# The last norm of a two-layer encoder: its sums, weights and stores taken apart

## The chip, the cores and the metric

The kernel runs on one core of one Trainium2 chip. The metric is the device time of one execution in microseconds (us). The kernel before takes 1240.49 us (median of 3 runs, 1240.41 to 1240.75).

## The reference

The input is x, 256 tokens of 2048 features. Layer 0 is a pre-norm layer with differential attention and a spatial gating branch, layer 1 a pre-norm recurrent layer; both add a residual. The change touches only what follows the last product:

```
y = (h * silu(z_c)) @ c_w_out          # 256 x 2688 times 2688 x 2048
x = x + y
return x * rsqrt(mean(x * x, axis=-1) + 1e-6) * final_norm
```

So each token needs the sum of the squares of all its 2048 features before any of its output can be scaled.

## The kernel before, in words

All weights stream from memory in the order of use, as chunks that are cut into units of up to eight 128x128 tiles. A unit is loaded by the queue of SP (`load`, line 204, tile `raw`), split by ACT into a high part (`split_hi`, `hi`) and by DVE into a low part (`split_lo`, `lo`), and multiplied by PE as three products (lines 337 to 339). Loads run six units ahead of the splits, and the splits up to six units ahead of the products.

`run(emit)` writes the program of one chunk s. `at(s, fn, ph)` puts other work into a chunk's program: phases -1 to 0.5 around the splits, 1 and 1.5 behind them, 2 behind the products. Each engine executes its own instructions in the order in which they were written, so a helper's place in that order decides what it waits behind. A DMA that SP or ACT issues is an instruction of that engine's queue too.

The last product, `out_product("co", KC, x2_done)`, goes over four blocks of 512 features (cb 0 to 3), each block as two accumulators, one for each half of the tokens (t = 0 and 1, 128 tokens on the 128 partitions). In the last chunk the products of t = 0 come first and those of t = 1 after them. When a block is done, `res_add` (line 382, DVE) adds the residual into `res`, and `squares` (line 385, ACT) squares the 512 features and leaves their sum in one column of `ssq`. For the first three blocks this runs beside the products of the next block, and `gf_mult` (line 986, DVE) multiplies the finished features by final_norm there. The weights of that norm, `gf`, are eight tiles of 256 features, which ACT's queue loads at chunk s1 + 8 (line 978), s1 being the first chunk of the last product.

The last block has no product behind it. For each half of the tokens the program does, in this order: `res_add`, `squares`, then `finish(t)`: DVE sums the four columns of `ssq` (line 362) and turns them into mean plus eps (line 366), POOL takes the power -1/2 (line 367), and then ACT scales features 0 to 511 and 512 to 1023 (line 1006), and DVE scales 1024 to 1535 (line 1008) and scales and weights the last 512 in two pieces of 256 (line 1012). SP stores four pieces of 512 features for each half (line 1013), eight stores in all.

Of the kernel before, what the change touches and what calls it, by code (L numbers as in the profile page):

```python
# [12 lines left out]
ALU = mybir.AluOpType  # L13
AX = mybir.AxisListType

P = 128
S = 256
NT = S // P
DM = 2048
# [7 lines left out]
EPS = 1e-6  # L27
# [43 lines left out]
def plan():  # L71

    chunks = []
    add = lambda kind, **kw: chunks.append(dict(kind=kind, **kw))
    for cb in range(4):
        for kq in range(4):
            add("vb", cb=cb, kq=kq, n=16)
    for ct in range(KD):
        add("u", ct=ct, n=16)
        add("zb", ct=ct, n=16)  # L80

    def heads(p):
        for h in (2 * p, 2 * p + 1):
            for j in range(2):
                add("q", h=h, j=j, n=16)
            for j in range(2):
                add("k", h=h, j=j, n=16)
        for kq in range(4):
            add("v", p=p, kq=kq, n=16)

    def za(p):
        for kq in range(4):
            add("za", p=p, kq=kq, n=16)

    def out(kind, rows):

        for cb in range(4):
            for k in range(0, rows - 3, 4):
                nk = rows - k if rows - k < 8 else 4
                add(kind, cb=cb, k0=k, nk=nk, n=4 * nk)  # L100

    heads(0)
    out("ob", KD)
    za(0)
    for p in range(1, H // 2):
        heads(p)
        za(p)
    out("oa", KD)

    early = [(j, k) for j in range(2) for k in range(12)] + [(j, k) for j in range(2) for k in range(12, KD)]  # L110
    xb = lambda jk: add("xb", jk=jk, n=16)
    xb(early[:16])
    xb(early[16:])
    for j in range(2, LEAD):
        xb([(j, k) for k in range(KD)])
    for j in range(KC):
        if j + LEAD < KC:
            xb([(j + LEAD, k) for k in range(KD)])
        for z in z_rows(j):
            add("zc", j=z, n=16)  # L120
        add("gt", j=j, n=2 * len(gate_tiles(j)))
    add("zc", j=KC - 1, n=16)
    out("co", KC)
    off = 0
    for c in chunks:
        c["off"] = off
        off += c["n"] * P * P
    return chunks, off
# [3 lines left out]
def trunk(ctx, tc, xT, xt, prm, rep, wsp, wst, out):  # L132
    nc = tc.nc
    V, A, T, GP, SP = nc.vector, nc.scalar, nc.tensor, nc.gpsimd, nc.sync
# [20 lines left out]
    mhalf = cpool.tile([P, NT], F32, name="mhalf")  # L155
    GP.memset(mhalf, -0.5)
    small = lambda n, w: cpool.tile([P, w], F32, name=n)
    rt, rh, nlam = small("rt", NT), small("rh", NT), small("nlam", 1)
# [7 lines left out]
    res = room.rearrange("p (t d) -> p t d", t=NT)  # L166
    ssq = small("ssq", NT * 4).rearrange("p (t c) -> p t c", t=NT)
# [22 lines left out]
    chunks, _ = plan()  # L190
# [70 lines left out]
    def at(s, fn, ph=0):  # L261


        assert (s, ph) > passed[0], (s, ph)
        todo.setdefault((s, ph), []).append(fn)
# [94 lines left out]
    def q_sum(ts=slice(0, NT)):  # L360

        V.tensor_reduce(rt[:, ts], ssq[:, ts, :], axis=AX.X, op=ALU.add)
        return rt[:, ts]

    def r_pow(ps, ts=slice(0, NT)):
        V.tensor_scalar(rt[:, ts], ps, 1.0 / DM, EPS, op0=ALU.mult, op1=ALU.add)
        GP.tensor_tensor(rt[:, ts], rt[:, ts], mhalf[:, ts], op=ALU.pow)
# [12 lines left out]
    def res_add(cb, pss, t):  # L380
        f = slice(cb * 512, (cb + 1) * 512)
        V.tensor_tensor(res[:, t, f], res[:, t, f], pss[t], op=ALU.add)

    def squares(cb, t):
        A.activation(sqs, res[:, t, cb * 512:(cb + 1) * 512], AF.Square, accum_out=ssq[:, t, cb:cb + 1])
# [69 lines left out]
    with tc.tile_pool(name="pb", bufs=2) as pb:  # L455
# [112 lines left out]
        for ct in range(KD):  # L568
            u = None
# [224 lines left out]
    with tc.tile_pool(name="pc", bufs=2) as pc:  # L794
        y.add(pc, KC - KD, "y2")
        tl = lambda n, j, b, dt=F32: pc.tile([P, S], dt, tag=n, name=f"{n}{j}", bufs=b)
# [176 lines left out]
        gf, s1 = [], pos[0]  # L973

        def gf_load():
            for a in range(DM // S):
                gf.append(tl("th" if a < 4 else "q", f"gf{a}_", 4))
                A.dma_start(gf[a], rep[:, GF + a * S:GF + (a + 1) * S])

        at(s1 + 8, gf_load)  # L980

        def gf_mult(cb):
            for t in range(NT):
                for a in (2 * cb, 2 * cb + 1):
                    r = res[:, t, a * S:(a + 1) * S]
                    V.tensor_tensor(r, r, gf[a], op=ALU.mult)

        def x2_done(cb, pss, s):
            if s < len(chunks) - 1:
                at(s + 1, lambda: [res_add(cb, pss, t) for t in range(NT)])  # L990
                at(s + 1, lambda: [squares(cb, t) for t in range(NT)], 1)
                at(max(s + 2, s1 + 10), lambda: gf_mult(cb), 1)
                return
            for t in range(NT):
                at(s, lambda t=t: (res_add(cb, pss, t), squares(cb, t), finish(t)), 2)

        def finish(t):


            ts = slice(t, t + 1)  # L1000
            r_pow(q_sum(ts), ts)
            sc = rt[:, ts]
            for n, (a, b) in enumerate(((0, 512), (1024, 1536), (512, 1024), (1536, 2048))):
                r = res[:, t, a:b]
                if n % 2 == 0:
                    A.activation(r, r, AF.Copy, scale=sc)
                elif b < DM:
                    V.tensor_scalar_mul(r, r, sc)
                else:
                    for c in range(a, b, S):  # L1010
                        r = res[:, t, c:c + S]
                        V.scalar_tensor_tensor(r, r, sc, gf[c // S], op0=ALU.mult, op1=ALU.mult)
                SP.dma_start(out[:, t, a:b], res[:, t, a:b])

        out_product("co", KC, x2_done)


# [89 lines left out]
```

## Time and profile before

| what | us |
|---|---|
| median of 3 runs | 1240.49 |
| the profiled execution | 1240.98 |
| its span, first to last instruction | 1239.2 |
| PE busy | 1228.1 (99% of the span) |
| DVE busy | 844.1 |
| ACT busy | 673.6 |
| POOL busy | 34.9 |

The span is the time between the first and the last instruction that the profiler recorded; the 1.8 us between it and the execution's time lie around it. A time in a row is counted from the span's start. An engine's busy time is an average over the whole program: PE is busy for 99% of it, and yet the last stretch, in which PE has nothing left to do, is ruled by other engines.

### The profile page before, as it was taken

How to read it: one execution, taken by the hardware profiler on the slowest of the kernel's cores; microseconds unless marked ns; L12 is line 12 of the kernel's file. 1: busy time of each engine (PE TensorE's matmuls, PEld its weight loads, DVE VectorE, ACT ScalarE, POOL GpSimd, SP SyncE). 2: the span in 40 equal slices, each digit the busy share in tenths (PEclk: the TensorE clock that was granted, in tenths of full speed). 3: DMA queues.
4: the chain of work that ended last, by engine and by line, in shares of the span. 5: the costliest groups of instructions: out<-in, count | busy, mean ns of one | idle time of the engine just before them, and what ended most of it. 6: DMA issues, size and time to landing. Idle time of an engine off the chain costs nothing.

```text
span 1239.2 us, 17358 instructions
## 1 busy us (share of the span) xinstructions
PE 1228.1 (99%) x6458; PEld 1056.9 (85%) x6458; DVE 844.1 (68%) x1304; ACT 673.6 (54%) x1083; POOL 34.9 (3%) x66
## 2 busy tenths in 40 slices
PE   9999999999999999999999999999999999999997
PEld 7888888888888888888888888888989989898885
DVE  6847777777556656746646655557899999988553
ACT  7544444454444334444544544455788788877442
POOL 1100000000000000000000000000000000000000
PEclk9999999999999999999999999999999999999999
DMA  9855665555645565555555555455566666656651
GB/s 329 278 188 170 238 202 173 186 187 176 213 156 187 193 196 172 187 170 174 184 174 167 191 174 179 170 189 172 202 192 198 215 205 203 207 179 228 223 178 68
DMA packets 70981, 237.66 MB, mean 192 GB/s; under 512 B 8176, under 2 KB 9840, under 8 KB 70640
## 3 DMA queue, kind: packets, MB, share of 16 engines
q1 hardware_dynamic: 66960, 228.76, 55.4%
q10 hardware_dynamic: 2016, 4.64, 1.1%
q0 software_dynamic: 1920, 3.15, 1.0%
q8 instruction: 51, 0.84, 0.3%
q14 instruction: 34, 0.28, 0.1%
HBM read 231.27 MB, written 2.10 MB: 188 GB/s over the span
## 4 chain that ended last, share of the span: by engine, by line
PE 98%; DMA 1%; DVE 0%; SPq 0%; issue 0%; ACT 0%; ACTq 0%; POOLq 0%; POOL 0%; DVEq 0%
PE ps_xb L320 6%; PE ps_zc L320 6%; PE ps_zb L320 5%; PE ps_k L320 5%; PE ps_q L320 5%; PE ps_u L320 5%; PE ps_zc L324 3%; PE ps_xb L324 3%; PE ps_co L339 3%; PE ps_co L337 3%; PE ps_co L338 3%; PE ps_q L324 2%; PE ps_u L324 2%; PE ps_k L324 2%; PE ps_zb L324 2%; PE ps_v L337 2%
## 5 line engine op out<-in xcount | busy, mean ns | idle before, releaser
L242 DVE TENSOR_TENSOR lo<-raw,hi 128x1024 fp32r<-128x1024 f32 (+2 forms) x425 | 502.1, 1199 | 181.7 <-ACT hi L228 172.2
L228 ACT CAST hi<-raw 128x1024 fp32r<-128x1024 f32 (+2 forms) x425 | 427.0, 1034 | 245.6 <-PE ps_za L339 49.7
L320 PE MATMUL ps_xb<-x,hi 128*128 128x512 f32 x336 | 84.4, 392 | 0.0
L320 PE MATMUL ps_zc<-x,hi 128*128 128x512 f32 x336 | 83.6, 391 | 0.0
L320 PEld LDWEIGHTS ps_zc<-x,hi 128*128 128x128 f32 x336 | 61.7, 188 | 11.8
L320 PEld LDWEIGHTS ps_xb<-x,hi 128*128 128x128 f32 x336 | 61.5, 188 | 11.0
L337 PE MATMUL ps_co<-hi,y 128*128 128x512 f32 x168 | 65.4, 389 | 0.0
L338 PE MATMUL ps_co<-lo,y 128*128 128x512 f32 x168 | 65.4, 389 | 0.0
L339 PE MATMUL ps_co<-hi,y 128*128 128x512 f32 x168 | 65.4, 389 | 0.0
L320 PE MATMUL ps_zb<-x,hi 128*128 128x512 f32 x256 | 65.0, 396 | 0.0
L320 PE MATMUL ps_q<-x,hi 128*128 128x512 f32 x256 | 63.7, 393 | 0.0
L320 PE MATMUL ps_u<-x,hi 128*128 128x512 f32 x256 | 63.7, 391 | 0.0
L320 PE MATMUL ps_k<-x,hi 128*128 128x512 f32 x256 | 63.4, 393 | 0.0
L320 PEld LDWEIGHTS ps_u<-x,hi 128*128 128x128 f32 x256 | 47.0, 188 | 9.1
L320 PEld LDWEIGHTS ps_q<-x,hi 128*128 128x128 f32 x256 | 47.1, 188 | 9.0
L320 PEld LDWEIGHTS ps_k<-x,hi 128*128 128x128 f32 x256 | 47.1, 188 | 8.9
L320 PEld LDWEIGHTS ps_zb<-x,hi 128*128 128x128 f32 x256 | 47.1, 189 | 8.5
L337 PE MATMUL ps_vb<-hi,x 128*128 128x512 f32 x128 | 51.1, 400 | 0.5 <-ACT hi L234 0.5
L338 PE MATMUL ps_vb<-lo,x 128*128 128x512 f32 x128 | 50.4, 393 | 0.7 <-DVE lo L235 0.7
L337 PE MATMUL ps_v<-hi,x 128*128 128x512 f32 x128 | 50.7, 396 | 0.0
L337 PE MATMUL ps_ob<-hi,y 128*128 128x512 f32 x128 | 50.6, 395 | 0.0
L337 PE MATMUL ps_za<-hi,x 128*128 128x512 f32 x128 | 50.4, 394 | 0.0
(299 smaller groups left out, 2363.3 us busy)
## 6 DMA issues: line engine op xcount, KB each, us to landing
raw<-in_wst SPq DMA_DIRECT2D x400, 512.0 KB, 4.1
raw<-in_wst SPq DMA_DIRECT2D x34, 256.0 KB, 5.7
raw<-in_wst SPq DMA_DIRECT2D x15, 384.0 KB, 3.1
res<-in_xt ACTq DMA_DIRECT2D x2, 1024.0 KB, 7.2
out_x<-res SPq DMA_DIRECT2D x8, 256.0 KB, 2.4
seam<-xcp POOLq DMA_DIRECT2D x9, 192.0 KB, 3.1
res<-in_xT SPq DMA_DIRECT2D x3, 512.0 KB, 6.7
seam<-xcp POOLq DMA_DIRECT2D x6, 128.0 KB, 2.9
```

The costliest lines, as they stand in the source:

```text
L228: A.copy(hi[:, :(b - a) * P], raw[u][:, :(b - a) * P])
L242: V.tensor_sub(lo[:, :n], raw[u][:, :n], hi[:, :n].bitcast(F32))
L320: wide = lambda i: T.matmul(ps, hi[:, col(tiles[i][0])], m.both[tiles[i][1]], start=first and i == 0, stop=last and i == n - 1)
L324: T.matmul(ps[:, :S], lo[:, col(w)], m.hi[k], start=False, stop=False)
L337: T.matmul(pss[t], mh, hi[:, s], start=a, stop=False)
L338: T.matmul(pss[t], mh, lo[:, s], start=False, stop=False)
L339: T.matmul(pss[t], ml, hi[:, s], start=False, stop=b)
```

## The change

Four things change, all in the last norm.

- The mean is left out: the weights `gf` are multiplied by sqrt(2048) after they are loaded (`gf_root`, eight DVE instructions at chunk s1 + 9), so that the sum of squares plus 2048 eps takes the place of the mean plus eps.
- The first three columns of `ssq` are summed, and 2048 eps added, in `sum_before` on DVE, two chunks after the third block, for both halves at once. `finish` then has one addition of the last column.
- The last 512 features are multiplied by their weights in two pieces of 256 right after `res_add`, into tiles of their own, written ahead of that addition. Later they are only scaled.
- The pieces to be scaled and stored are six for each half instead of four: ACT scales 0 to 511 and 512 to 767 and its own queue stores them; DVE scales 768 to 1279, 1280 to 1535 and the two weighted pieces, and SP stores these four.

```diff
         at(s1 + 8, gf_load)
+        def gf_root():
+
+            for g in gf:
+                V.tensor_scalar_mul(g, g, math.sqrt(DM))
+
+        at(s1 + 9, gf_root, 1)
...
+        before = small("before", NT)
+
+        def sum_before():
+
+            V.tensor_reduce(before, ssq[:, :, :3], axis=AX.X, op=ALU.add)
+            V.tensor_scalar_add(before, before, DM * EPS)
+
         def x2_done(cb, pss, s):
             if s < len(chunks) - 1:
...
                 at(max(s + 2, s1 + 10), lambda: gf_mult(cb), 1)
+                if cb == 2:
+                    at(s + 2, sum_before, 1.5)
                 return
...
         def finish(t):
-            ts = slice(t, t + 1)
-            r_pow(q_sum(ts), ts)
-            sc = rt[:, ts]
-            for n, (a, b) in enumerate(((0, 512), (1024, 1536), (512, 1024), (1536, 2048))):
-                r = res[:, t, a:b]
-                if n % 2 == 0:
+            last = []
+            for a in (6, 7):
+                last.append(tl("u", f"out{t}{a}_", 4))
+                V.tensor_tensor(last[-1], res[:, t, a * S:(a + 1) * S], gf[a], op=ALU.mult)
+            sc = rt[:, t:t + 1]
+            V.tensor_tensor(sc, ssq[:, t, 3:4], before[:, t:t + 1], op=ALU.add)
+            GP.tensor_tensor(sc, sc, mhalf[:, 0:1], op=ALU.pow)
+            row = lambda a, b: (res[:, t, a:b], a, b)
+            for n, (r, a, b) in enumerate((row(0, 512), row(768, 1280), row(512, 768), row(1280, 1536),
+                                           (last[0], 1536, 1792), (last[1], 1792, DM))):
+                if n in (0, 2):
                     A.activation(r, r, AF.Copy, scale=sc)
-                elif b < DM:
-                    V.tensor_scalar_mul(r, r, sc)
+                    A.dma_start(out[:, t, a:b], r)
                 else:
-                    for c in range(a, b, S):
-                        r = res[:, t, c:c + S]
-                        V.scalar_tensor_tensor(r, r, sc, gf[c // S], op0=ALU.mult, op1=ALU.mult)
-                SP.dma_start(out[:, t, a:b], res[:, t, a:b])
+                    V.tensor_scalar_mul(r, r, sc)
+                    SP.dma_start(out[:, t, a:b], r)
```

The instructions of DVE at the program's end, of the first half and the beginning of the second, before the change (a row gives line, operation, output and inputs, shape):

```order
L382 TENSOR_TENSOR res<-res,ps_co_0_11089 128x512
L362 TENSOR_REDUCE rt<-ssq 128x1
L366 TENSOR_SCALAR rt<-rt 128x1
L1008 TENSOR_SCALAR res<-res,rt 128x512
L1012 SCALAR_TENSOR_TENSOR res<-res,rt,qgf__10808 128x256
L1012 SCALAR_TENSOR_TENSOR res<-res,rt,qgf__10810 128x256
L382 TENSOR_TENSOR res<-res,ps_co_1_11090 128x512
```

The same stretch of DVE with the change; `uout` are the new tiles of the weighted features:

```order
L382 TENSOR_TENSOR res<-res,ps_co_0_11098 128x512
L1018 TENSOR_TENSOR uout__11274<-res,qgf__10809 128x256
L1018 TENSOR_TENSOR uout__11276<-res,qgf__10811 128x256
L1020 TENSOR_TENSOR rt<-ssq,before 128x1
L1029 TENSOR_SCALAR res<-res,rt 128x512
L1029 TENSOR_SCALAR res<-res,rt 128x256
L1029 TENSOR_SCALAR uout__11274<-uout__11274,rt 128x256
L1029 TENSOR_SCALAR uout__11276<-uout__11276,rt 128x256
L382 TENSOR_TENSOR res<-res,ps_co_1_11099 128x512
```

Two products stand ahead of the wait for the squares, one small instruction where two stood behind it, and four scalings where three stood, ahead of the second half's `res_add`.

ACT at the program's end with the change, from the first half's squares on (before, each half had its squares and two scalings of 512, and no DMA):

```order
L385 ACTIVATE sqr,ssq<-res 128x512
L1026 ACTIVATE res<-res,rt 128x512
L1027 DMA out_x<-res 128x512
L1026 ACTIVATE res<-res,rt 128x256
L1027 DMA out_x<-res 128x256
L385 ACTIVATE sqr,ssq<-res 128x512
```

Two DMA issues of the first half now stand ahead of the second half's squares in ACT's queue.

DVE at chunk s1 + 9 with the change; `thgf` and `qgf` are the eight tiles of `gf`:

```order
L242 TENSOR_TENSOR lo_10847<-raw_10728,hi_10846 128x1024
L983 TENSOR_SCALAR thgf__10797<-thgf__10797 128x256
L983 TENSOR_SCALAR thgf__10799<-thgf__10799 128x256
L983 TENSOR_SCALAR thgf__10801<-thgf__10801 128x256
L983 TENSOR_SCALAR thgf__10803<-thgf__10803 128x256
L983 TENSOR_SCALAR qgf__10805<-qgf__10805 128x256
L983 TENSOR_SCALAR qgf__10807<-qgf__10807 128x256
L983 TENSOR_SCALAR qgf__10809<-qgf__10809 128x256
L983 TENSOR_SCALAR qgf__10811<-qgf__10811 128x256
L242 TENSOR_TENSOR lo_10895<-raw_10762,hi_10894 128x1024
```

Between two `lo` splits that followed each other before there are now eight instructions, each of which waits for its tile's load.

## Rows read from the trace of the kernel before

**Rows 1.** The page: the span, and the chain's shares by engine.
```profile
span 1239.2 us, 17358 instructions
...
PE 98%; DMA 1%; DVE 0%; SPq 0%; issue 0%; ACT 0%; ACTq 0%; POOLq 0%; POOL 0%; DVEq 0%
```

**Rows 2.** Timeline, PE: the last product of each half (start, duration, engine, line).
```profile
1226.68 0.39 PE L339 MATMUL ps_co<-hi,y 128*128 128x512 f32 x1
...
1230.08 0.39 PE L339 MATMUL ps_co<-hi,y 128*128 128x512 f32 x1
```

**Rows 3.** Timeline, DVE, 1226.9 to 1235 us (in brackets: idle before, releaser).
```profile
1227.11 0.69 DVE L382 TENSOR_TENSOR res<-res,ps_co 128x512 f32<-128x512 f32 x1 [10.21 <-PE ps_co L339]
1228.65 0.16 DVE L362 TENSOR_REDUCE rt<-ssq 128x1 f32<-128x4 f32 x1 [0.85 <-ACT sqr L385]
1228.84 0.15 DVE L366 TENSOR_SCALAR rt<-rt 128x1 f32<-128x1 f32 x1
1229.69 0.48 DVE L1008 TENSOR_SCALAR res<-res,rt 128x512 f32<-128x512 f32 x1 [0.69 <-POOL rt L367]
1230.09 0.48 DVE L1012 SCALAR_TENSOR_TENSOR res<-res,rt,qgf__10808 128x256 f32<-128x256 f32 x1
...
1230.88 0.68 DVE L382 TENSOR_TENSOR res<-res,ps_co 128x512 f32<-128x512 f32 x1
1232.41 0.16 DVE L362 TENSOR_REDUCE rt<-ssq 128x1 f32<-128x4 f32 x1 [0.85 <-ACT sqr L385]
...
1233.42 0.49 DVE L1008 TENSOR_SCALAR res<-res,rt 128x512 f32<-128x512 f32 x1 [0.67 <-POOL rt L367]
```

**Rows 4.** Timeline, ACT, 1226.9 to 1235 us.
```profile
1229.68 1.34 ACT L1006 ACTIVATE res<-res,rt 128x512 f32<-128x512 f32 x2 [1.07 <-POOL rt L367]
1231.65 0.63 ACT L385 ACTIVATE sqr<-res 128x512 f32<-128x512 f32 x1 [0.63 <-DVE res L382]
...
1233.42 1.33 ACT L1006 ACTIVATE res<-res,rt 128x512 f32<-128x512 f32 x2 [1.04 <-POOL rt L367]
```

**Rows 5.** Timeline, SP's queue: first, fifth and eighth store issued.
```profile
1230.43 0.35 SPq L1013 DMA_DIRECT2D out_x<-res  x1
...
1234.17 0.33 SPq L1013 DMA_DIRECT2D out_x<-res  x1
...
1235.56 0.40 SPq L1013 DMA_DIRECT2D out_x<-res  x1
```

**Rows 6.** DMA, 1225 to 1240 us: busy tenths in 40 slices; packets, MB, share.
```profile
DMA  0000000000000000299999991039999999000000
...
q1 hardware_dynamic: 1152, 2.10, 37.4%
...
out_x<-res SPq DMA_DIRECT2D x8, 256.0 KB, 2.4
```

**Rows 7.** DMA, 1164 to 1168 us: ACT's queue, loads of gf in 1 KB rows.
```profile
q10 hardware_dynamic: 960, 0.88, 66.0%
```

**Rows 8.** Groups by form: instructions of the new shapes (busy, mean ns).
```profile
L665 DVE TENSOR_SCALAR e<-e,sm 128x256 f32<-128x256 f32 x8 | 2.8, 348 | 0.0
...
L986 DVE TENSOR_TENSOR res<-res,qgf__10804 128x256 f32<-128x256 f32 x2 | 0.8, 418 | 0.0
...
L858 ACT ACTIVATE q<-q 128x256 f32<-128x256 f32 x21 | 8.8, 418 | 0.7
```

**Rows 9.** Timeline, ACT, 1157 to 1172 us: last load of gf, a later split.
```profile
1166.15 0.44 ACTq L978 DMA_DIRECT2D qgf__10810<-in_rep  x1
...
1169.31 1.06 ACT L228 CAST hi<-raw 128x1024 fp32r<-128x1024 f32 x1 [0.60 <-PE ps_co L339]
```

**Rows 10.** Page, DMA issues: the same load, us to landing.
```profile
qgf__10810<-in_rep ACTq DMA_DIRECT2D x1, 128.0 KB, 5.4
```

**Rows 11.** Timeline, DVE, 1166 to 1176 us: the low part of that split.
```profile
1170.40 1.23 DVE L242 TENSOR_TENSOR lo<-raw,hi 128x1024 fp32r<-128x1024 f32 x1 [0.24 <-ACT hi L228]
```

**Rows 12.** Busy time by stretch: us, then PE, PEld, DVE, ACT, POOL.
```profile
1170.00:1180.00 10.00, 10.00 (x46) 8.27 (x45) 7.50 (x12) 5.92 (x9) 0.00 (x0) 1.00 0.73 240
```

More of the change, by code (lines that the diff above doesn't have):

```diff
@@ L997, in finish @@
         def finish(t):
-            ts = slice(t, t + 1)
-            r_pow(q_sum(ts), ts)
-            sc = rt[:, ts]
-            for n, (a, b) in enumerate(((0, 512), (1024, 1536), (512, 1024), (1536, 2048))):
-                r = res[:, t, a:b]
-                if n % 2 == 0:
+            last = []
[9 more added lines that the diff above has]
+                if n in (0, 2):
                     A.activation(r, r, AF.Copy, scale=sc)
-                elif b < DM:
+                    A.dma_start(out[:, t, a:b], r)
+                else:
                     V.tensor_scalar_mul(r, r, sc)
-                else:
-                    for c in range(a, b, S):
-                        r = res[:, t, c:c + S]
-                        V.scalar_tensor_tensor(r, r, sc, gf[c // S], op0=ALU.mult, op1=ALU.mult)
-                SP.dma_start(out[:, t, a:b], res[:, t, a:b])
+                    SP.dma_start(out[:, t, a:b], r)
         out_product("co", KC, x2_done)
```

## The prediction

> **What bounds the kernel now.** I began with the page. By the chain of the work that ended last, 98% of the span is PE [rows 1], and in the stretch of the last product PE is busy for 10.00 of 10 us [rows 12]. The change takes nothing from PE, so all it can move is the stretch in which PE is done. That stretch I read engine by engine in the timeline. The last product of the first half starts at 1226.68 and of the second at 1230.08 [rows 2], and DVE's residual addition of the first half begins 0.43 us after its product's start [rows 3]; so the second half's accumulator is ready at 1230.08 + 0.43 = 1230.51. From there to the end of the span at 1239.2 are 8.7 us, 0.7% of the whole. Within them the reader is to see three links.
>
> First, DVE is late: the second half's addition starts at 1230.88, not at 1230.51, because the first half's three scalings stand ahead of it [rows 3]. Second, a serial chain: addition 1230.88, squares on ACT 1231.65 [rows 4], sum on DVE 1232.41, mean, the power on POOL, scaling 1233.42. Third, the stores: the first of the second half is issued at 1234.17 and the last at 1235.56 [rows 5]. The DMA view shows what these do: in slices of 0.375 us the engines are full in two bursts, one of the first half (slices 16 to 24), one of the second (slices 26 to 33, the last full slice ending at 1237.75) [rows 6]. In between they are idle for about a slice and a half. The second burst is 1.05 MB, begins about 0.8 us behind the issue of its first store, and is full until it ends; so the end follows from when it begins and how many bytes it has. Behind it lie 1.45 us (1239.2 less 1237.75), which I keep.
>
> **The change part by part.**
>
> *Sum and mean.* The reduction and the mean (start to start 1228.65 to 1228.84 = 0.19 us) become one addition of 128x1 in place of two dependent instructions. I price the addition as the mean that it replaces (0.15 us) and so take off 0.19 us for each half. From sum to scaling were 1.04 us in the first half and 1.01 in the second [rows 3]; they become 0.85 and 0.82. `sum_before` adds two instructions of two columns, like the reduction and mean at 0.16 and 0.15, while PE works. They cost nothing.
>
> *Weights earlier.* Two products of 128x256 come in behind the addition. Such a product lasts 0.418 us [rows 8]; back to back, instructions of DVE start about 0.08 us before the previous one's recorded end (0.48 long, next start after 0.40 [rows 3]), so two take about 0.34 + 0.42 = 0.76 us. The cover is DVE's wait for the squares, 0.85 us [rows 3]. They just fit. If the cover were gone they would cost up to 0.76 us in each half; if they run over it by the 0.04 us that a dependent instruction waits, 0.
>
> *Scaling of the first half.* It starts at 1229.69 - 0.19 = 1229.50. DVE has one of 512 (next start 0.40 later) and three of 256. A scaling of 256 from a column lasts 0.348 us [rows 8], so 0.27 from start to start: 0.40 + 3 x 0.27 = 1.21 us, as long as the old three (1.19). The second half's addition starts at 1230.71, 0.17 earlier than before and still behind PE's 1230.51.
>
> *ACT's stores.* What is new here is a wait on ACT: each store waits for its own scaling, and behind the first half's two stores stand the second half's squares. Scaling 512 takes about 0.71 us (half of 1.34 plus the overlap [rows 4]) to 1230.21; the issue 0.33 to 0.44 us [rows 5, 9] and 0.04 on either side; scaling 256, 0.418 us [rows 8]; again an issue. ACT is free between 1231.45 and 1231.65. The squares could start 0.77 us behind the addition, as now (1230.88 to 1231.65), at 1231.48. Bounds: late by nothing, or by 0.17. I take 1231.50, near the shorter issues, since SP's stores are the same kind of transfer. Then the sum is at 1231.50 + 0.76 = 1232.26 and the scaling at 1233.08, 0.34 us earlier than 1233.42.
>
> *First store of the second half.* Before, it waited for ACT's 512 (issue 0.75 us behind the start of scaling). Now the first to be ready is DVE's 512: 0.49 + 0.04 = 0.53, so the issue comes at 1233.61, 0.56 us earlier than 1234.17.
>
> *The burst.* Bytes are unchanged. Issues don't limit it: SP spaces its stores by 0.46 us (1234.17 to 1235.56 in three steps), which puts its fourth at about 1235.0, and ACT's second is issued about 1234.7; at the same 0.8 us lag all bytes are available by 1235.8, while at the old rate the burst runs to 1237.2. What is unknown is the rate in rows of 1 KB, which half of the bytes now have. A 2 KB store takes 0.374 x 16 x 15 us / 1024 = 88 ns of an engine [rows 6], eight stores of 128 rows being 1024 of the 1152 packets. The nearest rows of 1 KB are loads: 0.66 x 16 x 4 us / 960 = 44 ns [rows 7], so no loss per byte. A burst of 256 packets of 2 KB and 512 of 1 KB is then (256 x 88 + 512 x 44) / 16 = 2.82 us, as 512 x 88 / 16 = 2.82 before. The bounds are, below, a burst so short that only the last issue sets the end (the third rival, 1.6 us gained), and above a price per packet that doesn't fall with size (88 ns: 4.22 us). I take 44 ns, the only row of this size.
>
> [...]
>
> *The weights' root.* Eight scalings of 256 in place take 8 x 0.27 = 2.2 us on DVE, behind loads the last of which is issued at 1166.15 and lands 5.4 us later, at 1171.55 [rows 9, 10]. They stand ahead of the split that runs at 1170.40 [rows 11], which then starts at about 1172.4 and ends at 1173.6. Its cover is the ring: ACT cast this unit's high part at 1169.31 because PE had just freed a place, so five units are still ahead of it; at 46 products in 10 us [rows 12] a unit of 12 is about 2.6 us, and with one of them half as long PE reaches it after some 12 us, at 1181. It has 7 to 8 us to spare. Cost 0; if the cover were gone, up to 3.2 us once (1173.6 less the old end).
>
> *Sum.* The end moves by 0.56 us if the burst keeps its length, and by 0.34 if it can make no use of the earlier first piece. I take 0.45 between them. The profiled execution, 1240.98 us with a span of 1239.2, would become 1240.53. It lies 0.49 above the median 1240.49, so the forecast is 1240.49 - 0.45 = 1240.04.
>
> **The rivals.**
>
> *Packets, not bytes (slower).* If a store's packet of 1 KB costs as much as one of 2 KB, each half's burst lasts 4.22 us. The first begins at 1230.06 (DVE's 512 of the first half) + 0.8 = 1230.86 and ends at 1235.08, after the second could begin; the two run as one to 1239.3 instead of 1237.75: 1.55 us later, 1242.0. It decides from the price at which the burst is 0.56 us longer: (256 x 88 + 512 p) / 16 = 3.38, p = 62 ns. For it: no store of this size is in the trace, and packets double on half of the bytes. Against it: the 44 ns of the loads.
>
> *ACT holds the squares.* With issues longer than the 0.44 us of [rows 9] by 0.1 or more, or a wait of the store behind its own scaling longer than on SP, the squares start 0.2 to 0.4 us late and eat the two savings in front of them. What is left is the first piece, 0.2 us or less: 1240.3 to 1240.5, no change. For it: ACT would be free only 0.03 us before it is needed. Against it: 0.44 us was measured beside the traffic of the weights, of which nothing is left at the end.
>
> *The burst gets shorter.* If two queues keep the engines fuller than one, or the last small store needs only its own time, the end is bounded by the last issue: 1235.0 + 0.8 + 128 KB at the old rate (0.35) = 1236.15, 1.6 us before 1237.75: 1238.9. Against it: the engines are already full in nine tenths and more of each slice [rows 6].
>
> *The root stalls PE.* Loads that land 8 us later than now would do it, and would cost what exceeds that, 1 to 3 us: up to 1243. The rows leave little room for it.
>
> **How the numbers follow.** Forecast as worked out (0.2 to 0.9 us gained): 0.62. ACT holds the squares: 0.16. Packets: 0.10, with every price between 62 and 88 ns. A shorter burst: 0.08. The root or anything unforeseen ahead of the last product: 0.04. The range 1239.2 to 1241.2 takes in the forecast, ACT's case, most of the shorter burst and the packets' case up to about 80 ns; what lies outside is under 0.2. A measurement of this kernel can tell a change from none at about 0.2%, 2.5 us. The whole stretch is 8.7 us and no case but the worst of PE's stall passes 2.5, so faster 0.02, within 0.95, slower 0.03.
>
> **What would show it right or wrong.** In the changed profile: the addition L1020 starts within 0.05 us of the squares' end and the two L1018 lie before it; from there to the scaling 0.82 to 0.85 us; the second `res_add` at about 1230.7 against a last product at 1230.08; the squares of the second half at 1231.5 (at 1231.7 and later, ACT's queue held them); the first store of the second half 0.5 to 0.6 us earlier relative to the last product; a second burst of 2.7 to 2.9 us (over 3.4 us the packets' rival holds, under 2.4 the shorter burst); PE without a gap at chunk s1 + 9. A time outside 1239.2 to 1241.2 would mean that something before the last product moved, and the forecast's ground would be wrong.

## The result: 18.7 us slower, and the profile after

The changed kernel takes 1259.23 us (median of 5 runs, 1258.85 to 1259.69) where the kernel before took 1240.49 beside it (1240.3 to 1240.75): ratio 1.0148, interval 1.0137 to 1.0159. The forecast was 1240.0, with 1239.2 to 1241.2 around it.

The page of the changed kernel answers to [rows 1]; its second row gives the busy time, share and instruction count of each engine:

```profile
span 1257.2 us, 17374 instructions
...
PE 1247.1 (99%) x6458; PEld 1054.6 (84%) x6458; DVE 848.0 (67%) x1318; ACT 672.2 (53%) x1083; POOL 34.8 (3%) x66
...
PE 98%; DMA 0%; SPq 0%; issue 0%; ACT 0%; DVE 0%; POOLq 0%; POOL 0%; ACTq 0%
```

The same row of the page before:

```profile
PE 1228.1 (99%) x6458; PEld 1056.9 (85%) x6458; DVE 844.1 (68%) x1304; ACT 673.6 (54%) x1083; POOL 34.9 (3%) x66
```

PE executes as many products (x6458) and is busy for 19.0 us longer. The view of waits says that it waits no longer than before (us in total, times, longest). The changed kernel:

```profile
PE warm L258 <- DVE ones L154: 1.1, 1, 1.1
PE ps_vb L338 <- DVE lo L235: 0.4, 2, 0.2
```

and the kernel before:

```profile
PE warm L258 <- DVE ones L154: 1.1, 1, 1.1
PE ps_vb L338 <- DVE lo L235: 0.7, 3, 0.2
PE ps_vb L337 <- ACT hi L234: 0.5, 1, 0.5
```

So the products themselves have become slower, and the groups by line say which. First before, then after (busy us, mean ns; 256 products each):

```profile
L320 PE MATMUL ps_k<-x,hi 128*128 128x512 f32 x256 | 63.4, 393 | 0.0
...
L324 PE MATMUL ps_k<-x,lo 128*128 128x256 f32 x256 | 33.2, 282 | 0.0
```

```profile
L320 PE MATMUL ps_k<-x,hi 128*128 128x512 f32 x256 | 64.5, 397 | 0.0
...
L324 PE MATMUL ps_k<-x,lo 128*128 128x256 f32 x256 | 32.9, 281 | 0.0
```

Products of 512 columns cost more, those of 256 a little less. The mean of one product hides most of it, since neighbours overlap (below, a product of 0.39 us at 103.53 is followed by the next at 103.76, 0.23 us later); what counts is the step from start to start. PE's timeline at one chunk of the first layer, before:

```profile
103.53 0.39 PE L320 MATMUL ps_zb<-x,hi 128*128 128x512 f32 x1
103.76 2.08 PE L324 MATMUL ps_zb<-x,lo 128*128 128x256 f32 x16
105.67 3.59 PE L320 MATMUL ps_zb<-x,hi 128*128 128x512 f32 x15
109.10 0.39 PE L320 MATMUL ps_u<-x,hi 128*128 128x512 f32 x1
```

and after:

```profile
105.17 0.40 PE L320 MATMUL ps_zb<-x,hi 128*128 128x512 f32 x1
105.41 2.06 PE L324 MATMUL ps_zb<-x,lo 128*128 128x256 f32 x16
107.30 3.66 PE L320 MATMUL ps_zb<-x,hi 128*128 128x512 f32 x15
110.80 0.40 PE L320 MATMUL ps_u<-x,hi 128*128 128x512 f32 x1
```

The reader is to subtract starts. Before, fifteen products of 512 take 109.10 - 105.67 = 3.43 us, 0.229 each; after, 110.80 - 107.30 = 3.50, 0.233 each. The sixteen of 256 take 1.91 before and 1.89 after. This is over 1000 us ahead of the first instruction that the change touches. The granted clock is 0.998 in both.

Averaged over the records of a kind, "wide" being line 320, "low" line 324, and "three" the sequences of lines 337 to 339 (steps between neighbours of one kind; longer pauses are left out, and so is the first step of each run of wide or low products):

```
kind             before    after    steps
wide, 512        228.2 ns  233.3    1425
low, 256         119.7     118.4    1478
three, 512       227.1     232.9    2360
```

The differences times the steps are +7.3, -1.9 and +13.7 us: 19.1, the whole of PE's 19.0.

What did change ahead of the norm is one line, which is in the diff but not among the four changes told ahead of the prediction: `small("before", NT)` reserves 32 bytes of each partition behind `rb` (8 are used), and everything that is reserved after it lies 32 bytes further on. The places in the two built programs (first byte in each partition; of the tiles that exist several times, the first place):

```
tile      x      y      rb      before   raw     hi      lo      second part of y
before    35488  68256  102048  -        105120  129696  154272  178848
after     35488  68256  102048  103072   105152  129728  154304  178880
```

Before, x, both parts of y, hi and lo lie a whole number of 4096 bytes apart. I call that distance 0. What one product reads begins at multiples of 512 bytes within these tiles, so that many differences between its two operands, all multiples of 512, are distance 0. After, hi, lo and y's second part are at distance 32 from x and y's first part, and still at distance 0 from each other.

**The last norm itself.** DVE, ACT and SP's queue of the changed kernel, to be held against [rows 3 to 5]:

```profile
1245.22 0.69 DVE L382 TENSOR_TENSOR res<-res,ps_co 128x512 f32<-128x512 f32 x1 [10.45 <-PE ps_co L339]
...
1246.76 0.16 DVE L1020 TENSOR_TENSOR rt<-ssq,before 128x1 f32<-128x1 f32 x1
1247.61 0.75 DVE L1029 TENSOR_SCALAR res<-res,rt 128x512 f32<-128x512 f32 x2 [0.69 <-POOL rt L1021]
...
1248.80 0.68 DVE L382 TENSOR_TENSOR res<-res,ps_co 128x512 f32<-128x512 f32 x1
...
1250.46 0.16 DVE L1020 TENSOR_TENSOR rt<-ssq,before 128x1 f32<-128x1 f32 x1 [0.18 <-ACT sqr L385]
1251.28 0.75 DVE L1029 TENSOR_SCALAR res<-res,rt 128x512 f32<-128x512 f32 x2 [0.67 <-POOL rt L1021]
```

```profile
1248.77 0.51 ACT L1026 ACTIVATE res<-res,rt 128x256 f32<-128x256 f32 x1 [0.43 <-ACT res L1026]
1249.31 0.35 ACTq L1027 DMA_DIRECT2D out_x<-res  x1
1249.70 0.63 ACT L385 ACTIVATE sqr<-res 128x512 f32<-128x512 f32 x1 [0.43 <-DVE res L382]
```

```profile
1251.80 0.81 SPq L1030 DMA_DIRECT2D out_x<-res  x2
...
1253.27 0.62 SPq L1030 DMA_DIRECT2D out_x<-uout__11296  x1
```

And its DMA view, 1243 to 1258 us, in the slices of [rows 6]:

```profile
DMA  0000000000000001999999950399999993000000
GB/s 0 0 0 0 0 0 0 0 0 0 0 0 0 0 0 38 350 393 388 328 344 382 374 200 0 109 377 399 355 336 355 380 372 115 0 0 0 0 0 0
```

Counted from the first half's addition (1227.11 before, 1245.22 after), the end comes at 1239.2 - 1227.11 = 12.09 and at 1257.2 - 1245.22 = 11.98 us: 0.11 earlier, where 0.45 was forecast. All of the loss lies before the norm.

The weights' root ran behind a wait of 0.34 us for its loads and ended at 1188.26; PE stayed full beside it and behind it, as in [rows 12]:

```profile
1187.14 0.29 DVE L983 TENSOR_SCALAR qgf__10805<-qgf__10805 128x256 f32<-128x256 f32 x1 [0.34 <-DMA qgf__10805<-in_rep]
...
1187.97 0.29 DVE L983 TENSOR_SCALAR qgf__10811<-qgf__10811 128x256 f32<-128x256 f32 x1
```

```profile
1180.00:1190.00 10.00, 10.00 (x45) 8.23 (x44) 5.55 (x13) 4.11 (x4) 0.00 (x0) 1.00 0.83 273
...
1188.00:1198.00 10.00, 10.00 (x45) 8.08 (x44) 8.53 (x12) 5.55 (x8) 0.00 (x0) 1.00 0.66 206
```

### The profile page after: what moved, and what is told of

It reads as the page before. It is cut to its first block, busy times and chain, and to the rows that moved or that the text cites. A ratio compares the mean times of both kernels' runs of the same rounds, so it can differ in the third digit from the quotient of the medians.

```text
span 1257.2 us, 17374 instructions
## 1 busy us (share of the span) xinstructions
PE 1247.1 (99%) x6458; PEld 1054.6 (84%) x6458; DVE 848.0 (67%) x1318; ACT 672.2 (53%) x1083; POOL 34.8 (3%) x66
## 4 chain that ended last, share of the span: by engine, by line
PE 98%; DMA 0%; SPq 0%; issue 0%; ACT 0%; DVE 0%; POOLq 0%; POOL 0%; ACTq 0%
PE ps_xb L320 6%; PE ps_zc L320 6%; PE ps_q L320 5%; PE ps_u L320 5%; PE ps_k L320 5%; PE ps_zb L320 5%; PE ps_xb L324 3%; PE ps_zc L324 3%; PE ps_co L337 3%; PE ps_co L339 3%; PE ps_co L338 3%; PE ps_zb L324 2%; PE ps_q L324 2%; PE ps_k L324 2%; PE ps_u L324 2%; PE ps_oa L339 2%
```

## The experiments

The theory: the distance in memory between what PE streams (x or y in the wide and low products, hi or lo in the three) and its stationary weights (the other of the two) sets the step. Its rivals: the new instructions or their order; the absolute place; the traffic of DMA, ACT and DVE into the moved tiles.

One test lies in the changed kernel itself. In the last product PE's stationary operand is y, first its first part and then its second; the streamed hi and lo are the moved ones for both. Twelve steps with the first part, and twelve with the second:

```profile
1206.83 0.39 PE L337 MATMUL ps_co<-hi,y 128*128 128x512 f32 x1
...
1209.63 0.39 PE L337 MATMUL ps_co<-hi,y 128*128 128x512 f32 x1
...
1215.82 0.39 PE L337 MATMUL ps_co<-hi,y 128*128 128x512 f32 x1
...
1218.54 0.39 PE L337 MATMUL ps_co<-hi,y 128*128 128x512 f32 x1
```

At distance 32 these are 2.80 / 12 = 0.233 us each, at distance 0 they are 2.72 / 12 = 0.227. Over the whole last product the steps average 233.3 ns with the first part (380 of them) and 227.0 with the second (116); in the kernel before both average 226.7. The same instructions, a few us apart, are slow or not by the place of one operand.

**1. Another size of the tile, and the move alone.** `e1_after_64`, against the changed kernel:

```diff
-        before = small("before", NT)
+        before = small("before", 16)[:, 0:NT]
```

> The changed kernel, but its new tile `before` takes 64 bytes of each partition instead of 32, so that all tiles behind it (the split weights `hi` and `lo`, the last tiles of `y`) lie 64 bytes behind their old place instead of 32. Address theory (a product of 512 columns takes 0.233 us instead of 0.227 when its two operands lie at different multiples of 32 within 64 bytes): PE is as fast as before, a product every 0.227 us, and what is left is the change of the tail, 0.1 to 0.5 us gained: 1240.0 to 1240.4. Code theory (the added instructions or the longer program slow PE): 1259, as the changed kernel.

Measured: 1245.42 us against 1241.02, ratio 1.0038 (1.0025 to 1.005). Neither number came. The same instructions as in the changed kernel are 13.8 us faster, so it isn't they that cost; but distance 64 isn't free. The same view as above:

```profile
104.53 1.98 PE L324 MATMUL ps_zb<-x,lo 128*128 128x256 f32 x16
106.35 3.65 PE L320 MATMUL ps_zb<-x,hi 128*128 128x512 f32 x15
109.84 0.40 PE L320 MATMUL ps_u<-x,hi 128*128 128x512 f32 x1
```

The wide step is that of distance 32 (3.49 / 15 = 0.233), while the sixteen low products take 1.82 us where they took 1.91: two opposite effects.

`e2_before_32`, the kernel before with the move and without a new instruction:

```diff
-    rb = cpool.tile([P, S], F32, name="rb")
+    rb = cpool.tile([P, S + 8], F32, name="rb")[:, 0:S]
```

> The kernel before, with the tile `rb` 32 bytes longer and nothing else: no instruction is added, but `hi`, `lo` and the last tiles of `y` move by 32 bytes, to the addresses that they have in the changed kernel. Address theory: 1259 (18.5 to 19 us slower), with products of 512 columns 0.233 us apart and those of 256 as before. Code theory: 1240.5, unchanged.

Measured: 1259.75, ratio 1.0151 (1.0136 to 1.0167). Its groups by line are those of the changed kernel to the digit:

```profile
L320 PE MATMUL ps_k<-x,hi 128*128 128x512 f32 x256 | 64.5, 397 | 0.0
...
L324 PE MATMUL ps_k<-x,lo 128*128 128x256 f32 x256 | 32.9, 281 | 0.0
```

The move alone makes the whole loss.

**2. Place or distance.** `e3_all_32` puts the 32 bytes ahead of x, so that everything moves together; `e4_x_32_hi_64` does this and the edit of e2 as well, so that x and y are moved by 32 and hi and lo by 64.

```diff
-    sp4, spn, spb = small("sp4", KC), small("spn", KC), small("spb", 1)
+    sp4, spn, spb = small("sp4", KC), small("spn", KC), small("spb", 9)[:, 0:1]
```

> The kernel before, with a small tile ahead of `x` 32 bytes longer: `x`, `y`, `hi` and `lo` all move by 32 bytes together. `hi` and `lo` are where they are in the changed kernel, but `x` and `y` lie at the same multiple of 32 within 64 bytes as they do. Address theory in its relative form: 1240.5, unchanged. In its absolute form (the split weights must not start at a multiple of 64): 1259.

> The kernel before, with `x` and `y` moved by 32 bytes and `hi`, `lo` and the last tiles of `y` by 64. The split weights lie at the same place within 64 bytes as in the kernel before, `x` and most of `y` do not. Relative form: 1259. Absolute form for the split weights: 1240.5. An order of operands that matters (the moving side must lie low) would show in which of the product groups slow down: those with `x` as the moving side (line 320) or those with the weights as the moving side (lines 337 to 339).

Measured: 1240.74, ratio 0.9999 (0.999 to 1.0008), and 1259.27, ratio 1.015 (1.0136 to 1.0164). Moving everything by 32 bytes does nothing that can be measured; moving hi and lo against x and y makes the whole loss.

**3. The changed norm with nothing moved.** `e5_after_unmoved` keeps the sums in spare columns of a tile that is there already:

```diff
-    rt, rh, nlam = small("rt", NT), small("rh", NT), small("nlam", 1)
+    rt, rh, nlam = small("rt", NT), small("rh", NT), small("nlam", 1 + NT)
...
+    nlam, before = nlam[:, 0:1], nlam[:, 1:1 + NT]
...
-        before = small("before", NT)
```

> The changed kernel with the new tile `before` put into the unused rest of an existing small tile's place, so that no tile moves: the change of the tail alone. Address theory: products of 512 columns 0.227 us apart as before, and the time 0.1 to 0.5 us below the kernel before (the tail of the changed kernel, from the first half's residual addition to the end of the span, was 11.98 us against 12.09). The rival, that part of the 18.7 us is in the added instructions (the weights' root, ACT's stores): 2 to 5 us slower than before, as e1 was (1245.4).

Measured: 1240.9 (11 runs) against 1240.96, ratio 1.0000 (0.9991 to 1.0009). The norm's change by itself is no difference that can be measured. Its end comes 12.07 us behind the first half's addition (12.09 before).

**4. Other distances.** `rb` longer by 32, 24, 64, 48 and 56 columns instead of 8: `e6_before_128`, `e7_before_96`, `e10_before_256`, `e12_before_192`, `e13_before_224`.

> The kernel before with `rb` 128 bytes longer: `hi`, `lo` and the last tiles of `y` move by 128 bytes against `x` and `y`. If only the place within 128 bytes counts, 1240.5 to 1241; if the distance itself counts (0 is best because both operands start in the same place of a larger pattern), 1244 to 1262.

> The kernel before with `rb` 96 bytes longer: distance 96 between the operands. If the pattern repeats every 64 bytes and odd multiples of 32 are bad, as 32 is: 1259. If it repeats every 128 bytes and falls off from 0: between e1's 1245 and 1260.

> The kernel before, with 256 bytes more behind rb: hi, lo and the second part of y lie 256 bytes further from x and the first part of y; no instruction is added. Distances 32, 96 and 128 cost 18 to 19 us alike, 64 costs 5. If only a distance that is a multiple of some hundred bytes is free and 256 is one, 1240.5; if every distance but none costs, 1258 to 1260. In the products: 228 or 233 ns apart for the wide ones.

> The kernel before with 192 bytes more behind rb (distance 192, which is 64 short of 256). If a distance and its complement to 256 act alike, the time is that of distance 64: 1245 (the 256-column products 115 ns apart, the wide ones 233). If what counts is how far the weights lie ahead, 1258 to 1260, as at 32, 96 and 128.

> The kernel before with 224 bytes more behind rb (distance 224, 32 short of 256). By the mirror 1259 as at distance 32; otherwise anything from 1235 to 1260, and below 1240 a better place than the one before.

Measured, with the steps by kind:

```
distance  kernel             us       ratio   interval          wide   low    three (ns)
0         before             -        1       -                 228.2  119.7  227.1
32        e2_before_32       1259.75  1.0151  1.0136 to 1.0167  233.3  118.4  233.0
64        e1_after_64        1245.42  1.0038  1.0025 to 1.005   233.4  115.3  228.9
96        e7_before_96       1260.13  1.0155  1.014 to 1.0171   234.3  118.1  233.1
128       e6_before_128      1258.93  1.0146  1.0132 to 1.016   232.7  118.6  232.4
192       e12_before_192     1250.84  1.0082  1.0065 to 1.0098  229.2  116.5  233.0
224       e13_before_224     1256.52  1.0127  1.0112 to 1.0142  233.2  116.8  232.9
256       e10_before_256     1240.96  1.0     0.999 to 1.0009   228.3  119.7  227.1
```

At 256 every step is that of 0. In between no time is as good, and 192 is neither 64 (1245) nor as bad as its neighbours, the miss of that run's expectations; it leaves the wide products nearly alone and slows the three, where 64 does the reverse. The steps agree once the distance has a direction. In the wide products the moved tiles are the weights, in the three they are what is streamed; so a move by 64 means "streamed less weights" = -64, that is 192 modulo 256, for the wide ones, and 64 for the three. The same steps (ns), put in that order:

```
streamed less weights   0      32     64     96     128    160    192    224
wide                    228.2  233.2  229.2  -      232.7  234.3  233.4  233.3
three                   227.1  233.0  228.9  233.1  232.4  -      233.0  232.9
```

Both kinds are fastest at 0, lose 1 to 2 ns at 64, and 4 to 6 ns at the others. The low products don't follow this: they gain a little at every distance between 0 and 256, most at 64. No distance tried beats 0 in all kinds.

**5. Only lo moved.** `e8_lo_32` and `e9_lo_64` put 32 and 64 bytes between hi and lo (8 and 16 columns):

```diff
-        hi, lo = parts[u] = ring(u, "hi", F32R), ring(u, "lo", F32R)
+        hi = ring(u, "hi", F32R)
+        if u == 0:
+            wpool.tile([P, 8], F32, tag="pad", name="pad", bufs=1)
+        lo = ring(u, "lo", F32R)
+        parts[u] = hi, lo
```

> The kernel before with 32 bytes between `hi` and `lo`: only `lo` (and the last tiles of `y`) move against `x`. Relative form: the products with `lo` as the moving side (line 338, 808 of them) take 6 ns longer, about 5 us in all, 1246, and those of line 320 (hi against x) keep 0.227. If the load of the next product's weights, not the product's own, is what collides with the moving side, the one product of line 320 that stands ahead of the 16 products with `lo` in each chunk is slow and the other 15 are not. If the whole group slows, 1259, the place of `hi` alone isn't what counts.

> The kernel before, with 64 bytes between the tiles hi and lo: hi keeps its place against x and y, lo and the second part of y lie 64 bytes further; no instruction is added. It asks whether the layout before is the best one. By the theory of the distance, the products of 256 columns with lo weights come 115 ns apart as at 64 bytes in e1_after_64 instead of 119.7 (some 1700 of them: -7.5 us), the wide products with hi weights stay at 228 ns, and the three-product sequences of the matrices take 229 ns in one product of three instead of 227 (+1 to +4 us). If the product ahead of a lo product pays as in e8_lo_32 (227 to 234 ns), some +4 to +8 us more. So 1237 to 1241 by the first, 1242 to 1246 by the second. A theory in which only the whole picture of addresses matters has no forecast below 1240.

Measured: 1251.61, ratio 1.0087 (1.0073 to 1.0101), and 1247.66, ratio 1.0055 (1.0042 to 1.0067): in both more than was expected of the simple reading. Where a wide product follows another, it keeps its 228.7 and 228.2 ns. Where a low product follows, whose weights have moved, the wide one goes from 226.8 to 234.9 in e8 (56 cases), but is at 226.1 in e9. Of the three, the product that streams lo takes 233.3 in e8, and its neighbours, which stream the unmoved hi, 230.5 and 231.7; in e9 all three take about 232. So at 32 these cases point to the weights to come, and the unmoved neighbours of a slow product are slow too, by 3 to 5 ns against the 227.1 of the kernel before. The changed kernel agrees where the last product goes from one part of y to the other. Of the four products at distance 32 whose successor's weights are at 0, three take 226 ns and one 233; the three at distance 0 whose successor's weights are at 32 take 235. e2, e4 and e15 give the same, within 1 ns. The timeline shows the load of the next weights (PEld, here for the product at 1212.42, the first with y's second part) beside the running product:

```profile
1212.20 0.39 PE L339 MATMUL ps_co<-hi,y 128*128 128x512 f32 x1
1212.20 0.19 PEld L337 LDWEIGHTS ps_co<-hi,y 128*128 128x128 f32 x1
1212.42 0.39 PE L337 MATMUL ps_co<-hi,y 128*128 128x512 f32 x1
```

A price for each pair of tiles, added up, doesn't give these numbers.

**6. PE without the traffic into its weights.** `e14_pe_alone` leaves out, from the seventh chunk on, the loads of the weights, the casts and the subtractions, and multiplies with what lies in the ring; `e15_pe_alone_32` is the same with the edit of e2. The core of the edit:

```diff
+        if c >= FINE:
+            parts[u] = kept[-RING:][u % RING]
+            return
         hi, lo = parts[u] = ring(u, "hi", F32R), ring(u, "lo", F32R)
-        if c >= FINE:
-            A.copy(hi[:, :(b - a) * P], raw[u][:, :(b - a) * P])
-            return
+        kept.append(parts[u])
```

> The kernel before, but from the seventh chunk on the loads of the large weights, their casts on ScalarE and their subtractions on VectorE are left out, and the products take the tiles that the first six chunks left in the ring (so the output means nothing). The distance is 0, as before. It is the base for e15_pe_alone_32. If PE's speed depended on the others' traffic, products come closer together than 228 ns (wide) and 120 ns (256 columns) and the time falls below 1230; if not, PE still sets the time at 1236 to 1240.

> As e14_pe_alone with 32 bytes more behind rb, so that the tiles hi and lo lie 32 bytes further from x and y. Theory A, the collision is between PE's own two reads: the wide products are 5 ns further apart than in e14_pe_alone (228 to 233), and the time is 17 to 19 us longer than its. Theory B, the collision is between PE's reads and the writes of DMA, ScalarE and VectorE into the moved tiles: with these gone the two kernels agree within 2 us.

Measured: 1240.68 (ratio 0.9999, 0.999 to 1.0009) and 1259.67 (ratio 1.0152, 1.0136 to 1.0167). The engines' rows of e14 and of e15, and PE's timeline of e15:

```profile
PE 1228.4 (99%) x6458; PEld 1057.2 (85%) x6458; DVE 362.3 (29%) x879; ACT 270.1 (22%) x658; POOL 31.1 (3%) x66
```

```profile
PE 1247.4 (99%) x6458; PEld 1054.6 (84%) x6458; DVE 362.5 (29%) x879; ACT 270.5 (21%) x658; POOL 31.2 (2%) x66
```

```profile
108.09 3.66 PE L322 MATMUL ps_zb<-x,hi 128*128 128x512 f32 x15
111.59 0.40 PE L322 MATMUL ps_u<-x,hi 128*128 128x512 f32 x1
```

DVE's work has fallen from 844 to 362 us and ACT's from 674 to 270, and yet the loss is 19.0 us, with the step of 3.50 / 15 = 0.233. Traffic into hi and lo is ruled out; DVE and ACT still write other tiles that moved, but beside the last product they do so for both parts of y alike. What is left is PE's own two readings: the streamed operand and the weights, which PEld loads beside the products. This is what the exclusions leave; no view shows the readings themselves.

**7. Four stores again.** `e11_four_stores`, against e5: DVE and SP take the pieces 0 to 511, 1024 to 1535 and the weighted 512 as one (in one tile; not shown), ACT 512 to 1023.

```diff
-            for n, (r, a, b) in enumerate((row(0, 512), row(768, 1280), row(512, 768), row(1280, 1536),
-                                           (last[0], 1536, 1792), (last[1], 1792, DM))):
-                if n in (0, 2):
+            for n, (r, a, b) in enumerate((row(0, 512), row(512, 1024), row(1024, 1536), (last, 1536, DM))):
+                if n == 1:
```

> As e5_after_unmoved (the change of the tail, nothing moved in memory), but with four stores of 512 features in each half instead of six: VectorE scales 0 to 512, 1024 to 1536 and the weighted last 512 (which lie in one tile) and SyncE stores them, ScalarE scales and stores 512 to 1024. It asks where the end's gain went: in e5_after_unmoved the first store of the second half came 0.48 us earlier, the end 0.02. If rows of 1 KB and two more stores with a late last issue took it, the burst is 2.7 us again and the last landing 1.45 us, and the end comes at 11.6 to 11.8 us behind the first half's addition (before 12.09, e5_after_unmoved 12.07). If the queues or the engines' rate set the end, it stays at 12.0 to 12.1. In time a few tenths of a us: 1240.1 to 1240.9 either way, so the profile decides.

Measured: 1240.15 us (11 runs) against 1240.97, ratio 0.9995 (0.9986 to 1.0004). Its end comes 11.42 us behind the first half's addition (1226.49), 0.67 earlier than before and 0.2 earlier than the prediction's 0.45 would have put it. SP's queue and the DMA view (1223.65 to 1238.65 us):

```profile
1232.89 0.81 SPq L1029 DMA_DIRECT2D out_x<-res  x2
1233.79 0.42 SPq L1029 DMA_DIRECT2D out_x<-out  x1
```

```profile
DMA  0000000000000000039999999019999999200000
GB/s 0 0 0 0 0 0 0 0 0 0 0 0 0 0 0 0 0 131 404 366 404 372 371 393 344 11 44 371 399 377 361 399 377 393 77 0 0 0 0 0
```

In its full slices the rate is 361 to 404 GB/s but for the last of the first burst (344), where the changed kernel falls to 328 to 355 in the middle of each burst. This is the best version tried: 1.5% below the changed kernel, and not to be told from the one before by its time, though its profile shows where two thirds of a microsecond went.

## Why the prediction was wrong

**The step that failed** is one sentence: "The change takes nothing from PE, so all it can move is the stretch in which PE is done." It counted instructions and left out where data lie. The `sum_before` paragraph priced two instructions rightly at nothing and not the tile that they write. By e2, a move of the tiles by its 32 bytes costs 18.7 us with no instruction added, since the step of the wide products goes from 228 to 233 ns and that of the three from 227 to 233; by e5, the rest costs nothing that can be measured. None of the four rivals has this mechanism; "anything unforeseen ahead of the last product" had 0.04 together with the root, which was priced at up to 1243, and "slower" had 0.03. The last sentence on what would show it wrong did hold: a time outside the range came from something before the last product.

The measurement decides: e14 and e15 differ in nothing but the 32 bytes behind `rb`, and take 1240.68 and 1259.67 us, 19.0 apart. In these products the step does depend on where the two operands lie.

**The steps on the norm**, from the first half's addition, in us:

```
                           before  forecast  after  e5_after_unmoved  e11_four_stores
second half's addition     3.77    3.60      3.58   3.58              3.58
second half's squares      4.54    4.39      4.48   4.48              4.30
second half's scaling      6.31    5.97      6.06   6.06              5.88
its first store issued     7.06    6.50      6.58   6.58              6.39
end of the span            12.09   11.64     11.98  12.07             11.42
```

- *Sum and mean, weights earlier, scaling of the first half: right.* The addition L1020 follows the squares at once, the scaling comes 0.82 to 0.85 us behind it, and the second half's addition is 0.19 earlier (forecast 0.17).
- *ACT holds the squares: in part.* ACT's queue was busy with its second store until 1249.66, and the squares began at 1249.70, 0.90 us behind the addition instead of 0.77. The rival's 0.2 to 0.4 was too much, the forecast's 0.02 too little: its issues were right (0.35), but the scaling of 256 took 0.51 where 0.418 was counted. e11, with one store less on ACT, has the squares at 4.30.
- *First store: right but for that wait*, 0.48 us earlier instead of 0.56.
- *The burst, mis-sized.* It still begins 0.84 us behind the first issue, but lasts about 2.85 us (from slice 25.7 to 33.3 of 0.375 us) against 2.74 in [rows 6], and in e5 about 2.96. By the packets' own records a store's packet of 1 KB took 46.7 ns on average in the changed kernel and 48.1 in e5, beside 88 for those of 2 KB: well under the 62 at which the packets' rival decides, but not 44. And 44 was misread. The 0.88 MB of [rows 7] in 960 packets average under 1 KB, since 103 of these packets have 4 bytes and took 9 ns; the 857 loads of 1 KB took 48.2, by which the prediction's own formula gives (256 x 88 + 512 x 48.2) / 16 = 2.95 us. The traces show the burst longer by about 0.11 us and, in e5, by 0.22.
- *The 1.45 us behind the burst, "which I keep": wrong.* They are now 1257.2 - 1255.49 = 1.71. With -0.48 + 0.11 + 0.26 the end moves by -0.11, as measured.
- In e11, with 2 KB rows and four stores, burst and remainder are back at 2.74 and 1.42, and the end moves by 0.67 us where its first store moves by 0.67. That the end follows from when the burst begins and how many bytes it has was right; which of row size, number of stores and last issue (0.62 us on SP where [rows 5] had 0.40) took the gain, these runs don't separate.
- *The root: cost 0, right*, though its last four loads came later than the DVE wanted them. Its price without cover was not 3.2 us: that counts from the split's old start, 1170.40; from the old end, 1171.63, to 1173.6 it is 2.0.
- Another reading was wrong without effect on the forecast: between the bursts of [rows 6] the engines are idle for about two and a half slices (tenths 1, 0 and 3), not one and a half.

**What stays open.** Which part of the memory or of PE makes the distance count, why 64 costs less than the others, why the low products gain, and why the neighbours of a slow product are slow too. In the runs the distance of its own operands doesn't settle a product's step alone. In lines 944 to 946, products of 256 columns, both operands move together; yet their 321 steps average 118.0 ns before and 115.7 in the changed kernel, where nine of the 21 groups average 113.3 and the others 117.8; in e3, which has all their operands at the same places as the changed kernel, they average 118.0. Distances that aren't a multiple of 32 were not tried.

## What to carry to other kernels

This kernel, in which PE is busy for 99% of the span, became 1.5% slower through a tile of 8 bytes: whenever a change adds or resizes a tile, compare the places of PE's two operands in the built programs, before and after, and put a new small tile where they keep their distance, as in spare columns of an old one (e5: ratio 1.0000). If a change slows products over the whole program with no new wait, look at starts, not at durations, and repeat the move without the change, as e2 does. And at an end that is bound by a burst of stores, see what a split into more and smaller stores costs: here, with six stores for each half (e5), a first store that came 0.48 us earlier moved the end by 0.02, and with four (e11) one that came 0.67 earlier moved it by 0.67.

## What the runs showed of the hardware

- The step from one fp32r product of 128x512 to the next, at granted clocks of 0.997 to 0.999, went in these runs by the distance in memory between the streamed operand and the stationary weights: 227 to 228 ns at 0 (the kernel before) and 256 bytes (e10), 229 where the streamed operand lies 64 bytes further, 256 counted as 0 (the three in e1, the wide in e12), 232 to 234 at the others tried (e2, e6, e7, e13, and the other kind in e1 and e12). The low products of 256 columns took 115.3 ns in e1 (hi and lo moved by 64 bytes) against 119.7 in the kernel before.
- At distance 32 the few cases that tell them apart point to the weights of the next product, which PEld loads beside the running one (at 1212.20 in the changed kernel): a product at distance 0 took 235 ns when its successor's weights were at 32 (three cases in each of four kernels; e8 has 234.9 in 56 cases).
- In these runs it was the distance and not the place (e3 1240.74 us, e4 1259.27; 233.3 against 227.0 ns by the part of y within the changed kernel), and it wasn't the traffic of other engines into hi and lo (e14, e15: 19.0 us apart with DVE's work more than halved, from 844 to 362 us, and no loads of large weights after the sixth chunk).
- A packet of 1 KB cost more per byte than one of 2 KB: stores took 46.7 ns in the changed kernel and 48.1 in e5 against 87 to 88, loads of 1 KB 48.2 in [rows 7]. The bursts that are half of 1 KB rows fell to 328 to 355 GB/s in the middle (the changed kernel, e5) where those of 2 KB rows kept 361 to 404 in all but one full slice (the kernel before, e11).
